# Layer B's last eight adaLN gate columns, made as sixteen half columns under the query projections

## The chip, the core and the metric

The kernel runs on one NeuronCore of one Trainium2 chip. The metric is device time in microseconds (us) of one launch. The kernel before took 1255.73 us in the median of three runs (1254.37, 1255.73, 1255.77).

## What is computed

A trunk of two layers on a sequence of 256 rows of width 2048, all in fp32. Layer A is a Mamba-2 mixer. Then one K and one V are projected for layer B, which is an attention over three head groups (dilations 1, 4 and 16) with its own queries and a SiLU gate path. Cut to what the change touches:

```python
for layer in range(2):
    shift, scale, gate = jnp.split(jax.nn.silu(c) @ ada_w[layer] + ada_b[layer], 3, axis=-1)
    h = x * (1.0 + scale) + shift
    y = _ssd_mixer(h, ...) if layer == 0 else _dilated_mixer(h, k_sh, v_sh, b_in_w[0], b_out_w[0])
    x = _layer_norm(4.0 ** 0.25 * x + (1.0 + gate) * y, ln_g[layer], ln_b[layer])
    if layer == 0:
        k_sh, v_sh = jnp.split(x @ kv_w, 2, axis=-1)     # 2048 -> 2 x 3072
```

The queries and z are `h @ b_in_w`, 2048 to 3072 + 1024. shift and scale are needed before the queries. gate is needed only behind the output projection, at the very end.

## The kernel before, in words

**A product.** Weights come from HBM in pieces of 128x1024 fp32 (512 KB). `load_piece` (L91) loads one into a buffer `raw`, of which there are six. `split` (L96) makes a high part `whi` on ScalarE (L99) and a low part `wlo` on VectorE (L101), four buffers each. TensorE multiplies both with the activations: `cm_wide` (L136) makes two 128-row tiles of K or of a query from four pieces, with matmuls of 512 columns on `whi` (L149) and 256 columns on `wlo` (L152); `tm_chunk` (L184) makes a 512-column stripe of V from eight pieces (L173 to L175). A buffer `raw` is free again when its `whi` and `wlo` are made, and the pair is free when TensorE has used it.

**adaLN.** A row of `ada_w` for 128 outputs, a column in the kernel's words, is a 128x2048 tile (1 MB) in one of two buffers `araw`. `ada_dot` (L246) multiplies it with silu(c) on VectorE (L251) and sums along the row, which gives one column of `mod`. Layer B has 48 columns: 16 pairs of scale and shift, then 16 of gate. `queue` (L269) turns a list of columns into background jobs: job i issues the load of column i+1 (L244) and then does the dot of column i. `background(n, every)` (L107) is called after each piece and runs n jobs per `every` pieces, so `rate` sets the mix. `gate_out` (L258) adds the bias to the gates, transposes them on TensorE (L262), copies the result on VectorE (L264) and stores it to DRAM (L265), from where the last stage reads it back spread over all partitions.

**The stages around the change.** Eleven of the 48 columns are done under layer A's output projection. The stage in `with tc.issue_after(tile4.ins)` makes the last V stripe of the first half, then the six K blocks (48 pieces), then three V stripes (24 pieces): 80 pieces in all, with R = (1, 2), one job per two pieces, for the other 37 columns and `gate_out(1)`. Then the activations are scaled and shifted in place (L828, L829, `split_act` L195), and `queries(0)` (L854), 24 pieces, makes the first half's queries. Under them run sixteen jobs `weigh` (L839), one per piece, which multiply the residual `u` with LayerNorm's g and add its b; each group of four loads 2x256 KB of `lnrow` spread over all partitions into one single buffer `pT` first. `attend(0)` (L861) and `queries(1)` follow and are interleaved on TensorE; in each of four heads come the scores (L874, L876), the bias (L880), the maximum (L883), the exponential on ScalarE (L885), its scaling (L887), the transposes (L890) and the product with V (L897, L900).

**What sets the order.** All loads are issued by one in-order queue, SP's. Every engine runs its instructions in the order in which the framework's list scheduler has put them; it lets an instruction move ahead of others where its own estimates and the buffers allow it. `issue_after(x)` keeps an instruction behind x.

Of the kernel before, what the change touches and what calls it, by code (L numbers as in the profile page):

```python
# [9 lines left out]
F32 = mybir.dt.float32  # L10
# [3 lines left out]
ALU = mybir.AluOpType  # L14
# [4 lines left out]
P = 128  # L19
L = 256  # L20
D = 2048
KT = D // P
# [7 lines left out]
EPS = 1e-5  # L30
SCALE = 128.0 ** -0.5
NEG = -1.0e30
SLOPES = [2.0 ** (-8.0 * n / 24.0) for n in range(1, 25)]


# [14 lines left out]
def trunk(ctx, tc, xT, x, c, par, cst, bias, lnrow, ada, wdt, win, wxs, wout, wk, wv, wbin, wbout, out):  # L50
    nc = tc.nc
    V, S, T, PO = nc.vector, nc.scalar, nc.tensor, nc.gpsimd

    cons = ctx.enter_context(tc.tile_pool(name="cons", bufs=1))
    wp = ctx.enter_context(tc.tile_pool(name="wp", bufs=3))
# [10 lines left out]
    cb_ = cons.tile([P, D], F32, name="cb_")  # L66
# [24 lines left out]
    def load_piece(src):  # L91
        raw = wp.tile([P, 1024], F32, name="raw", bufs=6)
        nc.sync.dma_start(raw, src)
        return raw
# [9 lines left out]
    jobs, latest, copied, pin = [], [], [], [None]  # L104

    def background(n, every=1):

        state[0] += n
        while state[0] >= every and jobs:
            state[0] -= every  # L110
            jobs.pop(0)()
# [17 lines left out]
    def acc_pair(pool=None):  # L129
        return [(pool or mm).tile([P, 2, L], F32, name="acc") for _ in range(2)]  # L130
# [8 lines left out]
    def cm_wide(src, dst, rate=(0, 1), moving=None):  # L139

        both, high = moving or (lambda kt: xp[:, kt], lambda kt: xhi[:, kt, :])
        ps = acc_pair()
        for q in range(KT // 4):
            hi, lo = (t.rearrange("p k n -> p (k n)").rearrange("p (k n) -> p k n", k=4)
                      for t in split(load_piece(src[q])))
            for k in range(4):
                kt = 4 * q + k
                for n in range(2):
                    T.matmul(ps[n], hi[:, k, n * P:n * P + P], both(kt), start=kt == 0, stop=False,  # L149
                             skip_group_check=True)  # L150
                for n in range(2):
                    T.matmul(ps[n][:, 0, :], lo[:, k, n * P:n * P + P], high(kt), start=False, stop=kt == KT - 1,  # L152
                             skip_group_check=True)
            background(*rate)
        for n in range(2):
            S.activation(dst[:, n, :], ps[n][:, 1, :], AF.Copy)
            V.tensor_tensor(dst[:, n, :], ps[n][:, 0, :], dst[:, n, :], op=ALU.add)

    def tiles(ps):
        return [ps[n // 2][:, n % 2, :] for n in range(4)]  # L160
# [71 lines left out]
    mod = [cons.tile([P, KT, 3], F32, name=f"mod{i}") for i in range(2)]  # L232
# [25 lines left out]
    def gate_out(layer):  # L258

        ada_bias(layer, slice(0, KT), slice(2, 3))  # L260
        pt = aux.tile([P, 512], F32, name="aux")[:KT, :P]
        T.transpose(pt, mod[layer][:, :, 2], ident)  # L262
        row = sm.tile([KT, P], F32, name="row", bufs=1)
        V.tensor_copy(row, pt)  # L264
        nc.sync.dma_start(gated[layer].rearrange("(k p) -> k p", p=P), row)  # L265

    def queue(pool, cols):

        loaded = [ada_load(pool, *cols[0])]  # L269

        def step(i):
            raw = loaded.pop(0)
            if i + 1 < len(cols):
                loaded.append(ada_load(pool, *cols[i + 1]))
            ada_dot(*cols[i], raw)

        jobs.extend(lambda i=i: step(i) for i in range(len(cols)))

    def drain():
        while jobs:  # L280
            jobs.pop(0)()
# [8 lines left out]
    with ExitStack() as cA:  # L290
# [14 lines left out]
        with ExitStack() as cS:  # L305
# [38 lines left out]
            def xs_wide(g):  # L344

                xs[g] = p0.tile([P, 4, L], F32, name="xs")
                for w in range(2):
                    t = xs[g][:, 2 * w:2 * w + 2, :]
                    cm_wide(wxs[2 * g - 4 + w], t, rate=R, moving=(lambda kt: hp[:, :, kt, :], hh_))
                    for n in range(2):  # L350
                        conv(t[:, n, :], 4 * g + 2 * w + n, t[:, n, :])

            def product(kind, g, pre=None):
# [7 lines left out]
                if kind == "z":  # L361
                    ps = tm_chunk(src, hh_, hl_, rate=R, k0=k0, pre=pre)
                    if g not in sz:
# [5 lines left out]
                    return  # L369
                ps = cm_quad(src, hhi, hlo, rate=R, k0=k0)  # L370
                t = tiles(ps)
# [9 lines left out]
            with ExitStack() as c0:  # L381
# [4 lines left out]
                raws, xts, late = [], {}, []  # L386
# [34 lines left out]
                part = {n: p[1:] for n, p in zip(names, begun.values())}  # L421
                two = "h"
                order = []
                for row in ("b4:0. b6:0. h z2:0. b2:0 x1:0 h", "b2:1. x1:1. z1:0 z1:1. z4:0 h h",
# [3 lines left out]
                    for w in row.split():  # L428
                        if w == two:
                            n = -2 if sum(o[0] == -2 for o in order) == sum(o[0] == -1 for o in order) else -1  # L430
# [98 lines left out]
            px = pe = cS.enter_context(tc.tile_pool(name="px", bufs=2, reuse_waits="tile"))  # L529
            R = (1, 10)  # L530

# [181 lines left out]
        cols1 = [(1, kind, kt) for kt in range(KT) for kind in ("scale", "shift")] + \  # L713
# [70 lines left out]
    with ExitStack() as cL:  # L784
        pl = cL.enter_context(tc.tile_pool(name="pl", bufs=3))

        vps = [tm_pair(), tm_pair()]
        for b in range(2):
            for kt in range(4):
                tile4 = x_tile(kt, (b,))  # L790
            for n in range(1, 4):
                normalise(b, 512 * n, 512 * n + 512)
            for i, w in enumerate(first_v):
                if b and i == 2:
                    x_tile(4)
                    x_tile(5)
                tm_mults(i // 2, w, vps[i % 2], hx, lx, 0, KT, (b,))
        for q in range(2, KT // 2):
            if q < KT // 2 - 1:
                x_tile(2 * q + 2)  # L800
                x_tile(2 * q + 3)
            for j in range(2):
                w = split(load_piece(wv[2 * j][q]), after=tile4.ins if q == 2 else None)
                tm_mults(q, w, vps[j], hx, lx, 0, KT, range(2))
        for g in range(2):
            evict_v(0, g, vps[g])

        R = (1, 2)
        pin[0] = latest[-1].ins
        with tc.issue_after(tile4.ins):  # L810
            state[0] = 0
            queue(pl, cols1[11:])
            jobs.append(lambda: gate_out(1))
            evict_v(0, 2, tm_chunk(wv[4], hx, lx, rate=R))
            for hq in range(2):
                for g in range(NG):
                    kv[hq, g] = place(3 + 3 * hq + g, [P, 4, L])
                    for w in range(2):
                        cm_wide(wk[2 * (2 * g + hq) + w], kv[hq, g][:, 2 * w:2 * w + 2, :], rate=R)
            for g in range(NG):  # L820
                evict_v(1, g, tm_chunk(wv[1 + 2 * g], hx, lx, rate=R))
            drain()
            late = latest[-1].ins

        ada_bias(1, slice(0, KT), slice(0, 2))
        for kt in range(KT):
            t = pl.tile([P, L], F32, name="htmp")
            S.activation(t, xhi[:, kt, :].bitcast(F32), AF.Identity, bias=shift(1, kt), scale=scale(1, kt))  # L828
            V.scalar_tensor_tensor(t, xlo[:, kt, :].bitcast(F32), scale(1, kt), t, op0=ALU.mult, op1=ALU.add)  # L829
            split_act(xhi[:, kt, :], xlo[:, kt, :], t)  # L830
    cQ = ctx.enter_context(ExitStack())
    pc2 = cQ.enter_context(tc.tile_pool(name="pc2", bufs=2))
# [5 lines left out]
    R = (0, 1)  # L838

    def weigh(n, b, i):  # L840
        if b == 0 and i == 0:
            t = pc2.tile([P, 1024], F32, name="pT", bufs=1)
            lnr[n] = [t[:, 512 * j:512 * j + 512] for j in range(2)]
            for j in range(2):
                bcast(lnr[n][j], lnrow, j * D + 512 * n)
        cs_ = slice(512 * n, 512 * n + 512)
        with tc.issue_after(late):
            V.tensor_tensor(u[b][:, cs_], u[b][:, cs_], lnr[n][i], op=(ALU.mult, ALU.add)[i])

    lnr = {}  # L850
    state[0] = 0
    jobs.extend(lambda n=n, b=b, i=i: weigh(n, b, i) for n in range(4) for i in range(2) for b in range(2))

    def queries(hq):  # L854
        qq = [pc2.tile([P, 4, L], F32, name=f"q{g}") for g in range(NG)]
        for g in range(NG):
            for w in range(2):
                cm_wide(wbin[2 * (2 * g + hq) + w], qq[g][:, 2 * w:2 * w + 2, :], rate=(1, 1))
        return qq

    def attend(hq, qq):  # L861

        for i in range(4):
# [3 lines left out]
            for g, c_ in enumerate((slice(0, 384), slice(384, 512), slice(512, 640))):  # L867
                V.scalar_tensor_tensor(bi[:, c_], dmat if g == 0 else dmat[:, P:2 * P], SLOPES[g * H + h], gmask[:, c_],
                                       op0=ALU.mult, op1=ALU.add)
# [59 lines left out]

    qs = [queries(0)]  # L930
    attend(0, qs[0])
    qs.append(queries(1))
    attend(1, qs[1])
    state[0] = 0
    jobs.extend(lambda i=i: hold(i, [hold_in(i, k) for k in range(2)]) for i in range(6))
# [102 lines left out]
def _layout(x, c, ada_w, ada_b, ln_g, ln_b, a_in_w, a_conv_w, a_conv_b, a_dt_bias,  # L1038
# [29 lines left out]
    def mask(delta, win_, dil):  # L1068
        return np.where((delta >= 0) & (delta % dil == 0) & (delta <= win_), 0.0, NEG)

# [37 lines left out]
```

## Time and profile before

| what | before |
|---|---|
| median of three runs | 1255.73 us |
| the profiled execution | 1254.31 us, of which the span is 1252.5 us |
| TensorE matmuls busy (PE) | 97% of the span |
| TensorE weight loads (PEld) | 83% |
| VectorE (DVE) | 82% |
| ScalarE (ACT) | 56% |
| mean rate of the DMAs | 268 GB/s |
| granted TensorE clock | 0.998 |

How to read it: times in the trace are counted from the start of the span. `L101` is line 101 of the kernel. A row of the timeline has start, duration, engine, line, operation, tiles, shapes and count, and in brackets the idle time of the engine just before it and what ended it. Durations of rows with x2 are from the first start to the last end.

### The profile page before, as it was taken

The numbers are of one execution on the slowest core, as the hardware profiler recorded it, in microseconds if no ns is written. First come the engines' busy times: TensorE is split into PE (matmuls) and PEld (weight loads), VectorE is DVE, ScalarE is ACT, GpSimd is POOL, SyncE is SP. The second block draws the span as 40 slices with busy tenths as digits, with TensorE's granted clock in tenths as the row PEclk, the third lists the DMA queues.
The fourth block names the chain that finished last, engine by engine and source line by source line (L and its number), as shares of the span: only waits on it lengthen the run. The fifth ranks groups of instructions, "written<-read, shape, count | busy, mean of one in ns | idle before, by whom it ended". The sixth has DMA issues, their size and how long they took to land.

```text
span 1252.5 us, 18746 instructions
## 1 busy us (share of the span) xinstructions
PE 1218.5 (97%) x7086; PEld 1042.7 (83%) x7086; DVE 1032.4 (82%) x1466; ACT 702.1 (56%) x1039; POOL 0.2 (0%) x4
## 2 busy tenths in 40 slices
PE   4999999999999999999999999999999999999997
PEld 4989998898888878788888788888888888888886
DVE  6999986999987989899777778879888866758777
ACT  3655577869588789653444444434445644445631
POOL 0000000000000000000000000000000000000000
PEclk9999999999999999999999999999999999999999
DMA  9999977677556546699898569989998774464741
GB/s 381 422 421 423 420 252 261 225 274 286 201 169 225 171 159 202 223 328 358 335 323 298 174 192 383 363 315 344 364 389 309 229 248 136 132 203 120 228 177 67
DMA packets 80586, 335.88 MB, mean 268 GB/s; under 512 B 9104, under 2 KB 9328, under 8 KB 67696
## 3 DMA queue, kind: packets, MB, share of 16 engines
q1 hardware_dynamic: 80496, 334.69, 73.9%
q8 instruction: 55, 0.90, 0.3%
q14 instruction: 35, 0.29, 0.1%
HBM read 332.47 MB, written 2.18 MB: 267 GB/s over the span
## 4 chain that ended last, share of the span: by engine, by line
PE 86%; DVE 5%; DMA 5%; issue 2%; ACT 1%; SPq 0%; DVEq 0%; ACTq 0%
PE acc L149 20%; PE acc L174 13%; PE acc L175 13%; PE acc L173 13%; PE acc L152 10%; PE acc L125 3%; PE acc L127 3%; PE acc L126 3%; DMA raw<-in_wk 2%; DVE wlo L101 1%; PE py L625 1%; DMA raw<-in_win 1%; DVE araw L251 1%; DMA araw<-in_ada 1%; DMA raw<-in_wv 1%
## 5 line engine op out<-in xcount | busy, mean ns | idle before, releaser
L99 ACT ACTIVATE whi<-raw 128x1024 fp32r<-128x1024 f32 x392 | 412.1, 1058 | 386.0 <-PE acc L175 151.4
L101 DVE TENSOR_TENSOR wlo<-raw,whi 128x1024 fp32r<-128x1024 f32 x392 | 473.5, 1221 | 145.3 <-ACT whi L99 141.1
L149 PE MATMUL acc<-actT,whi 128*128 128x512 f32 x1280 | 405.2, 397 | 0.0
L152 PEld LDWEIGHTS acc<-actT,wlo 128*128 128x128 f32 x1280 | 238.9, 188 | 62.8 <-DVE wlo L101 8.2
L174 PE MATMUL acc<-wlo,actT 128*128 128x512 f32 x688 | 270.0, 392 | 0.6 <-DVE wlo L101 0.5
L173 PE MATMUL acc<-whi,actT 128*128 128x512 f32 x688 | 266.6, 394 | 1.2 <-ACT actT L681 1.2
L152 PE MATMUL acc<-actT,wlo 128*128 128x256 f32 x1280 | 253.7, 280 | 4.5 <-DVE wlo L101 3.7
L251 DVE SCALAR_TENSOR_TENSOR araw<-araw,cb__72 128x2048 f32<-128x2048 f32 x96 | 219.3, 2285 | 9.5 <-DMA araw<-in_ada 9.3
L149 PEld LDWEIGHTS acc<-actT,whi 128*128 128x128 f32 x1280 | 195.8, 189 | 0.4
L175 PE MATMUL acc<-whi,actT 128*128 128x512 f32 x432 | 168.8, 391 | 0.0
L174 PEld LDWEIGHTS acc<-wlo,actT 128*128 128x128 f32 x688 | 129.3, 188 | 28.5 <-DVE wlo L101 2.8
L173 PEld LDWEIGHTS acc<-whi,actT 128*128 128x128 f32 x688 | 128.8, 188 | 27.2 <-ACT actT L681 1.7
L125 PE MATMUL acc<-actT,whi 128*128 128x256 f32 x384 | 108.9, 288 | 17.6 <-ACT actT L414 17.5
L126 PE MATMUL acc<-actT,whi 128*128 128x256 f32 x384 | 109.5, 287 | 0.0
L127 PE MATMUL acc<-actT,wlo 128*128 128x256 f32 x384 | 107.3, 287 | 1.2 <-DVE wlo L101 1.2
L175 PE MATMUL acc<-whi,ylo 128*128 128x512 f32 x256 | 100.7, 393 | 0.0
L175 PEld LDWEIGHTS acc<-whi,actT 128*128 128x128 f32 x432 | 81.1, 188 | 16.6
L125 PEld LDWEIGHTS acc<-actT,whi 128*128 128x128 f32 x384 | 74.3, 194 | 18.6 <-ACT actT L414 17.7
L126 PEld LDWEIGHTS acc<-actT,whi 128*128 128x128 f32 x384 | 75.1, 196 | 0.3
L127 PEld LDWEIGHTS acc<-actT,wlo 128*128 128x128 f32 x384 | 73.9, 196 | 1.6 <-DVE wlo L101 1.6
L175 PEld LDWEIGHTS acc<-whi,ylo 128*128 128x128 f32 x256 | 48.1, 188 | 9.7
L583 ACT ACTIVATE seg<-cbc,cumT 128x128 f32<-128x128 f32 x128 | 41.2, 389 | 5.0 <-PE py L625 4.9
(257 smaller groups left out, 1061.7 us busy)
## 6 DMA issues: line engine op xcount, KB each, us to landing
araw<-in_ada SPq DMA_DIRECT2D x96, 1024.0 KB, 7.3
raw<-in_win SPq DMA_DIRECT2D x112, 512.0 KB, 6.1
raw<-in_wout SPq DMA_DIRECT2D x64, 512.0 KB, 5.2
raw<-in_wbin SPq DMA_DIRECT2D x64, 512.0 KB, 4.2
raw<-in_wxs SPq DMA_DIRECT2D x48, 512.0 KB, 4.5
raw<-in_wv SPq DMA_DIRECT2D x48, 512.0 KB, 5.9
raw<-in_wk SPq DMA_DIRECT2D x48, 512.0 KB, 8.0
cbc<-cumd SPq DMA_DIRECT2D x16, 512.0 KB, 5.1
```

The source lines that it names most:

```text
L99: copied.append(S.activation(hi, raw, AF.Copy))
L101: latest.append(V.tensor_tensor(lo, raw, hi.bitcast(F32), op=ALU.subtract))
L125: T.matmul(o, hi[:, k, c_], ahi[:, kt, :], start=first, stop=False, skip_group_check=True)
L126: T.matmul(o, hi[:, k, c_], alo[:, kt, :], start=False, stop=False, skip_group_check=True)
L127: T.matmul(o, lo[:, k, c_], ahi[:, kt, :], start=False, stop=kt == k1 - 1, skip_group_check=True)
L149: T.matmul(ps[n], hi[:, k, n * P:n * P + P], both(kt), start=kt == 0, stop=False, skip_group_check=True)
L152: T.matmul(ps[n][:, 0, :], lo[:, k, n * P:n * P + P], high(kt), start=False, stop=kt == KT - 1, skip_group_check=True)
L173: T.matmul(o, h_, hi[:, k, :], start=kt == k0, stop=False, skip_group_check=part)
L174: T.matmul(o, h_, lo[:, k, :], start=False, stop=False, skip_group_check=part)
L175: end = T.matmul(o, l_, hi[:, k, :], start=False, stop=kt == k1 - 1, skip_group_check=part)
L251: V.scalar_tensor_tensor(raw, raw, 1.0, cb_, op0=ALU.mult, op1=ALU.mult, accum_out=mod[layer][:, ct, j:j + 1])
L583: S.activation(seg[:, hh, b, :], cbc[:, hh, b, :], AF.Relu, bias=cumT[:, b, h0 + hh:h0 + hh + 1], scale=-1.0)
```

## The change

The last eight of the sixteen gate columns leave the list of the K and V stage, and `gate_out(1)` with them. The other 29 columns of that stage run at R = (2, 5), two jobs per five pieces instead of one per two. The eight columns are loaded as sixteen halves of 128x1024 (512 KB) into the weight pieces' six buffers `raw`. Their jobs `half_dot` each issue the load of the next half and do the dot of their own. Eight of them stand between the `weigh` jobs of `queries(0)`, one after every two, so the `weigh` jobs now take 24 pieces; the other eight and `late_gates`, which adds the two partial sums and calls `gate_out(1)`, run in `queries(1)` with one job per two pieces. What is computed stays the same. Line numbers of the changed kernel are one higher up to L806, and about 26 higher from `queries` on.

```diff
+LATE = 8
...
-        R = (1, 2)
+        R = (2, 5)
         pin[0] = latest[-1].ins
         with tc.issue_after(tile4.ins):
             state[0] = 0
-            queue(pl, cols1[11:])
-            jobs.append(lambda: gate_out(1))
+            queue(pl, cols1[11:-LATE])
...
+    part = pc2.tile([P, LATE, 2], F32, name="part", bufs=1)
+    coming = []
+
+    def half_load(i):
+        raw = wp.tile([P, 1024], F32, name="raw", bufs=6)
+        nc.sync.dma_start(raw, ada[1, 2, KT - LATE + i // 2][:, 1024 * (i % 2):1024 * (i % 2) + 1024])
+        coming.append(raw)
+
+    def half_dot(i):
+        if i == 0:
+            half_load(0)
+        if i + 1 < 2 * LATE:
+            half_load(i + 1)
+        raw = coming.pop(0)
+        with tc.issue_after(late):
+            V.scalar_tensor_tensor(raw, raw, 1.0, cb_[:, 1024 * (i % 2):1024 * (i % 2) + 1024], op0=ALU.mult,
+                                   op1=ALU.mult, accum_out=part[:, i // 2, i % 2:i % 2 + 1])
+
+    def late_gates():
+        V.tensor_tensor(mod[1][:, KT - LATE:, 2], part[:, :, 0], part[:, :, 1], op=ALU.add)
+        gate_out(1)
+
     state[0] = 0
-    jobs.extend(lambda n=n, b=b, i=i: weigh(n, b, i) for n in range(4) for i in range(2) for b in range(2))
-
-    def queries(hq):
+    todo = [lambda n=n, b=b, i=i: weigh(n, b, i) for n in range(4) for i in range(2) for b in range(2)]
+    halves_ = [lambda i=i: half_dot(i) for i in range(2 * LATE)]
+    for i in range(8):
+        jobs.extend([*todo[2 * i:2 * i + 2], halves_[i]])
+    jobs.extend([*halves_[8:], late_gates])
+
+    def queries(hq, rate=(1, 1)):
...
-                cm_wide(wbin[2 * (2 * g + hq) + w], qq[g][:, 2 * w:2 * w + 2, :], rate=(1, 1))
+                cm_wide(wbin[2 * (2 * g + hq) + w], qq[g][:, 2 * w:2 * w + 2, :], rate=rate)
...
-    qs.append(queries(1))
+    qs.append(queries(1, (1, 2)))
+    drain()
```

SP's queue in the K projection before, with `raw` the weight pieces and `araw` the columns:

```order
L93 DMA raw_7573<-in_wk 128x1024
L93 DMA raw_7595<-in_wk 128x1024
L244 DMA araw_7617<-in_ada 128x2048
L93 DMA raw_7620<-in_wk 128x1024
L93 DMA raw_7642<-in_wk 128x1024
L244 DMA araw_7664<-in_ada 128x2048
```

and the same place of the queue now:

```order
L94 DMA raw_7570<-in_wk 128x1024
L94 DMA raw_7592<-in_wk 128x1024
L245 DMA araw_7614<-in_ada 128x2048
L94 DMA raw_7617<-in_wk 128x1024
L94 DMA raw_7639<-in_wk 128x1024
L94 DMA raw_7667<-in_wk 128x1024
L245 DMA araw_7689<-in_ada 128x2048
```

A column stood between every two pieces, and stands now in turn behind two and behind three.

VectorE at the start of `queries(0)` before: `wlo` are the low parts of the query weights, the rows with `u` are `weigh`, and the rows with `q0` evict the first two query tiles.

```order
L101 TENSOR_TENSOR wlo_9457<-raw_9454,whi_9456 128x1024
L868 SCALAR_TENSOR_TENSOR bi_9944<-bs_9342 128x384
...
L848 TENSOR_TENSOR u0_5509<-u0_5509,pT_9375 128x512
L848 TENSOR_TENSOR u1_5510<-u1_5510,pT_9375 128x512
...
L101 TENSOR_TENSOR wlo_9483<-raw_9480,whi_9482 128x1024
L101 TENSOR_TENSOR wlo_9506<-raw_9503,whi_9505 128x1024
L101 TENSOR_TENSOR wlo_9529<-raw_9526,whi_9528 128x1024
L157 TENSOR_TENSOR q0_9348<-acc_9351,q0_9348 128x256
...
L848 TENSOR_TENSOR u0_5509<-u0_5509,pT_9476 128x512
```

The same place now, where the rows with `part` are the halves:

```order
L866 SCALAR_TENSOR_TENSOR raw_9395,part_9314<-raw_9395,cb__72 128x1024
L102 TENSOR_TENSOR wlo_9432<-raw_9429,whi_9431 128x1024
L866 SCALAR_TENSOR_TENSOR raw_9397,part_9314<-raw_9397,cb__72 128x1024
L102 TENSOR_TENSOR wlo_9455<-raw_9452,whi_9454 128x1024
L866 SCALAR_TENSOR_TENSOR raw_9474,part_9314<-raw_9474,cb__72 128x1024
L848 TENSOR_TENSOR u0_5509<-u0_5509,pT_9346 128x512
L848 TENSOR_TENSOR u1_5510<-u1_5510,pT_9346 128x512
...
L158 TENSOR_TENSOR q0_9319<-acc_9322,q0_9319 128x256
...
L102 TENSOR_TENSOR wlo_9480<-raw_9477,whi_9479 128x1024
L102 TENSOR_TENSOR wlo_9506<-raw_9503,whi_9505 128x1024
L866 SCALAR_TENSOR_TENSOR raw_9554,part_9314<-raw_9554,cb__72 128x1024
L848 TENSOR_TENSOR u0_5509<-u0_5509,pT_9499 128x512
```

Three halves have come ahead of the first group of `weigh`, and that group stands now behind the low part of the sixth piece (`wlo_9455`), where it stood behind that of the fifth.

VectorE in the first head of `attend(0)` before, with `sc0` and `sc1` the scores of the two row blocks, `nm` their maximum and `den` the sums of the exponentials:

```order
L883 TENSOR_REDUCE nm_9954<-sc0_9948 128x1
L883 TENSOR_REDUCE nm_9973<-sc1_9967 128x1
L868 SCALAR_TENSOR_TENSOR bi_9995<-bs_9342 128x384
...
L886 RECIPROCAL den_9956<-den_9956 128x1
L887 TENSOR_SCALAR sc0_9948<-sc0_9948,den_9956 128x512
L886 RECIPROCAL den_9975<-den_9975 128x1
L887 TENSOR_SCALAR sc1_9967<-sc1_9967,den_9975 128x512
```

and now:

```order
L909 TENSOR_REDUCE nm_9951<-sc0_9945 128x1
L909 TENSOR_REDUCE nm_9970<-sc1_9964 128x1
L894 SCALAR_TENSOR_TENSOR bi_9992<-bs_9312 128x384
...
L866 SCALAR_TENSOR_TENSOR raw_10340,part_9314<-raw_10340,cb__72 128x1024
L912 RECIPROCAL den_9953<-den_9953 128x1
L913 TENSOR_SCALAR sc0_9945<-sc0_9945,den_9953 128x512
L912 RECIPROCAL den_9972<-den_9972 128x1
L913 TENSOR_SCALAR sc1_9964<-sc1_9964,den_9972 128x512
```

One half stands now between the maximum and the scaling of the first head; the next one (`raw_10393`) stands likewise ahead of the scaling of the fourth head.

## The prediction

> **What bounds the kernel now.** I read the page first, for the engine that is busiest, then the table of stretches by stage, then what TensorE's weight loads wait for, since a busy PE can hide waits.
>
> ```profile
> PE 1218.5 (97%) x7086; PEld 1042.7 (83%) x7086; DVE 1032.4 (82%) x1466; ACT 702.1 (56%) x1039; POOL 0.2 (0%) x4
> ```
>
> PE is busy 97% of the span, so only the places where it stands still can give anything back. The change touches the K and V stage and the queries. These are the stretches from the start of K to the end of `queries(1)`: us, then busy time with counts in the order PE, PEld, DVE, ACT, POOL, then clock, DMA share and GB/s.
>
> ```profile
> 776.00:843.00 67.00, 67.00 (x387) 58.44 (x386) 53.27 (x54) 26.41 (x34) 0.00 (x0) 1.00 0.90 345
> 843.00:912.00 69.00, 67.32 (x379) 56.83 (x378) 60.21 (x64) 29.57 (x39) 0.00 (x0) 1.00 0.95 357
> 912.00:979.00 67.00, 66.83 (x293) 53.96 (x292) 57.16 (x72) 39.25 (x58) 0.00 (x0) 1.00 0.87 331
> 979.00:999.00 20.00, 20.00 (x115) 17.37 (x114) 14.32 (x20) 10.63 (x15) 0.00 (x0) 1.00 0.73 218
> 999.00:1019.00 20.00, 19.29 (x109) 16.24 (x108) 14.86 (x19) 8.52 (x11) 0.00 (x0) 1.00 0.77 234
> 1019.00:1050.00 31.00, 31.00 (x181) 27.16 (x181) 17.74 (x20) 13.85 (x18) 0.00 (x0) 1.00 0.69 233
> 1050.00:1081.00 31.00, 31.00 (x203) 27.57 (x201) 28.34 (x65) 15.39 (x32) 0.00 (x0) 1.00 0.28 89
> 1081.00:1132.00 51.00, 51.00 (x295) 44.52 (x294) 25.96 (x28) 22.35 (x27) 0.00 (x0) 1.00 0.60 191
> ```
>
> The first two rows hold the same work, K. In the first, PE does 387 matmuls in 67 us, 5.776 per us, and never stops. At that rate 69 us would hold 398.6; the second row has 379. The 19.6 that are missing are 3.4 us. Row five has 109 where 20 us would hold 115.5: 1.1 us. The waits of the weight loads say for what, in these three windows (843 to 912, 912 to 960, 1000 to 1020; total, times, longest):
>
> ```profile
> PEld acc L152 <- DVE wlo L101: 4.3, 6, 1.4
> ...
> PEld acc L174 <- DVE wlo L101: 1.7, 4, 0.5
> ...
> PEld acc L152 <- DVE wlo L101: 1.6, 2, 0.8
> ```
>
> TensorE waits for the low parts that VectorE makes, and in the K and V stage at a steady beat:
>
> ```profile
> 849.07 0.30 PEld L152 LDWEIGHTS acc<-actT,wlo 128*128 128x128 f32 x2 [0.59 <-DVE wlo L101]
> 860.63 0.30 PEld L152 LDWEIGHTS acc<-actT,wlo 128*128 128x128 f32 x2 [0.58 <-DVE wlo L101]
> 872.99 0.30 PEld L152 LDWEIGHTS acc<-actT,wlo 128*128 128x128 f32 x2 [1.38 <-DVE wlo L101]
> ```
>
> Six waits of 4.3 us cost 3.4 us, so about 0.15 us of each is the ordinary spacing of two loads. The four of the V stripes then cost 1.7 - 4 x 0.15 = 1.1 us. Together the K and V stage loses 4.5 us and the queries 1.1 to 1.3.
>
> Why is VectorE late? A piece is 16 matmuls, 16 / 5.776 = 2.77 us, and 0.524 MB; a column is 1.049 MB. Two pieces and a column per 5.54 us are 2.097 MB, a need of 378 GB/s. The rows above deliver 345 and then 357 GB/s, the latter with the DMAs 0.95 busy. In the first 67 us the stage lives on what was loaded ahead: 67 x (378 - 345) = 2.2 MB, four pieces of the six buffers. From 843 us on the lead is gone. SP's queue adds to it: it issues a column only when a buffer is free, and the weights stand behind it.
>
> ```profile
> SPq L244 <- DVE araw L251: 145.5, 34, 7.5
> ```
>
> That is 145.5 us of SP waiting between 740 and 1050 us for the dot of an earlier column.
>
> **K and V stage: columns at two per five pieces.** The need falls to 5 x 0.524 + 2 x 1.049 = 4.72 MB per 13.85 us, 341 GB/s, a tenth less and just under what both stretches delivered. VectorE: the dots are 2285 ns and an accumulator read of 82 ns each.
>
> ```profile
> L251 DVE SCALAR_TENSOR_TENSOR araw<-araw,cb__72 128x2048 f32<-128x2048 f32 x96 | 219.3, 2285 | 9.5 <-DMA araw<-in_ada 9.3
> L101 DVE TENSOR_TENSOR wlo<-raw,whi 128x1024 fp32r<-128x1024 f32 x392 | 473.5, 1221 | 145.3 <-ACT whi L99 141.1
> ...
> L251 DVE DVE_READ_ACCUMULATOR araw<-araw,cb__72 128x1 f32 x34 | 2.8, 82 | 0.0
> ```
>
> Between 843 and 912 us stand 12 of them; a fifth fewer is 2.4 x 2.37 = 5.7 us, so DVE falls from 60.21 to 54.5 us of 69, 79%: the share of the first row (53.27 of 67), in which nothing waits. The last of the 29 jobs comes at piece 73 of 80, as the 37th did at 74, so the conversion of the activations behind it keeps its place. What could be late next there is the supply itself, 341 against 345 to 357 GB/s. Bounds for this term: nothing gone (0) to all gone (-4.5 us); I take **-4.5**, because the lead now lasts: even at 331 GB/s, the lowest of the three rows, the shortfall of 10 GB/s over 204 us is 2.0 MB, which the lead of four pieces covers.
>
> The store of the gates leaves this stage too. SP stood 10.7 us at it with the last weights of V behind it, and PE did not notice (row three loses only the 1.1 us above). I give nothing for it.
>
> ```profile
> SPq L265 <- DVE row L264: 10.7, 1, 10.7
> ```
>
> **First queries: eight halves, and `weigh` spread out.** The loss of 1.1 to 1.3 us comes from `weigh`: VectorE stands at it until its `lnrow` has landed, and the next `wlo` is behind it.
>
> ```profile
> 1003.94 1.29 DVE L848 TENSOR_TENSOR u<-u,pT 128x512 f32<-128x512 f32 x2 [1.17 <-DMA pT<-in_lnrow]
> 1006.65 0.69 DVE L848 TENSOR_TENSOR u<-u,pT 128x512 f32<-128x512 f32 x1 [1.41 <-DMA pT<-in_lnrow]
> 1007.26 1.22 DVE L101 TENSOR_TENSOR wlo<-raw,whi 128x1024 fp32r<-128x1024 f32 x1
> ...
> 992.43 0.80 SPq L63 DMA_DIRECT2D pT<-in_lnrow  x2
> 993.56 2.60 SPq L93 DMA_DIRECT2D raw<-in_wbin  x3
> 1000.53 1.44 SPq L63 DMA_DIRECT2D pT<-in_lnrow  x2
> ```
>
> With one buffer `pT`, load, `weigh` and next load form a ring that takes 1000.53 - 992.43 = 8.1 us and has four pieces, 11.1 us, at one job per piece. The jobs take one and a half times the pieces now, so the ring has 16.6 us, and the order puts 4 to 5 us of other work (two or three `wlo`, a half, the evictions) between a group's end and the next group's start. This wait should go: **-1.1** (bounds -1.3 and, if the halves only take its place, 0).
>
> The halves themselves: no such instruction is in the trace. Above, it costs like a `wlo` of the same 1024 columns plus the accumulator read, 1.30 us; below, half a dot plus the read, 1.22. I take 1.30. Eight are 10.4 us, so DVE between 979 and 1050 us goes from 46.9 to 57.3 us of 71. DMA: in the first 40 us, 9.0 MB moved at a share of 0.75; five halves add 2.6 MB and the last `lnrow` group (0.5 MB) moves out, so the share rises to 0.92. Full, but not over; and since a half uses one of the six buffers, the weights run about four pieces, 11 us, ahead, against 4.2 us for a piece to land:
>
> ```profile
> araw<-in_ada SPq DMA_DIRECT2D x96, 1024.0 KB, 7.3
> ...
> raw<-in_wbin SPq DMA_DIRECT2D x64, 512.0 KB, 4.2
> ```
>
> I take 0 for the halves here; without that cover, each half that delays a piece costs 0.524 MB at 299 GB/s (218 / 0.73), 1.75 us.
>
> The Trainium skill speaks against halves: its page "DMA: Bandwidth & Descriptors" asks in the section Bandwidth for transfers of 1 MiB or more, and gives in Anatomy of one DMA a fit, made on GpSimd's path, of about 2.0 us plus bytes / 436e3 for each. By it, as an estimate, sixteen halves would take 51 us one after another where eight columns take 35; if all of that showed, the sum would be 16 us worse. The trace agrees in direction (7.3 us for 1024 KB, 4.2 for 512), but not that it adds up: 357 GB/s were moved with both sizes in flight at once.
>
> **First attention: halves on a full VectorE.** Between 1050 and 1081 us DVE is busy 28.34 of 31 us, and two halves (2.6 us) come in. The one of the first head stands ahead of its scaling, with nothing else behind which it could hide:
>
> ```profile
> 1048.92 1.23 DVE L101 TENSOR_TENSOR wlo<-raw,whi 128x1024 fp32r<-128x1024 f32 x1 [1.56 <-PE aux L876]
> 1050.06 0.75 DVE L157 TENSOR_TENSOR q<-acc,q 128x256 f32<-128x256 f32 x2
> ...
> 1053.11 0.95 DVE L868 SCALAR_TENSOR_TENSOR bi<-bs 128x384 f32<-128x384 f32 x3
> 1053.98 0.16 DVE L886 RECIPROCAL den<-den 128x1 f32<-128x1 f32 x1
> ...
> 1054.76 0.49 DVE L887 TENSOR_SCALAR sc<-sc,den 128x512 f32<-128x512 f32 x1
> ...
> 1055.65 0.60 PE L890 MATMUL po<-cc,sc 128*128 128x128 f32 x4
> ```
>
> Scaling ends at 1055.25. PE comes to the first transposes at 1055.65, and by the changed order 0.4 us later, so there are 0.4 to 0.8 us of room. Its turn would be 1053.98. Its load stands behind that of a piece whose buffer the `wlo` of 1048.92 frees at 1050.15; issued at about 1050.5 and 4.2 us on its way, it lands at 1054.7. The scaling then ends 0.7 + 1.3 = 2.0 us later, less the room of 0.8 and another 0.5 since the two row blocks are transposed one after the other: **+0.7 us** (bounds 0, if the load is there, and 2.0 with no room). In the fourth head PE has some 3 us of query matmuls ahead of the transposes, which cover the other half. The gate's transposes, its copy and its store come late in `queries(1)`, before a stage that reads the store some 60 us later: 0.
>
> **Sum.** -4.5 - 1.1 + 0.7 = **-4.9 us**: the profiled execution of 1254.31 us would be 1249.4. The three runs are at 1254.4, 1255.7 and 1255.8, so that execution lies near the lowest; from their mean of 1255.3 I forecast **1250.4 us**.
>
> **Rivals.** (1) The waits under the queries only change their place: DMA at 0.92, `weigh` 0 instead of -1.1 and attention at 1.6: -2.9, 1252.4 us. For it: the share; against: four pieces of lead. (2) The change doesn't do what it says: VectorE's waits stay, since 341 GB/s is hardly less than what came, and only the queries gain: -1.1 + 0.7 = -0.4, 1254.9 us. For it: the first row moved no more than 345; against: it did so while SP waited for dots, and without PE losing anything. (3) Slower: VectorE stands at halves that have not landed, in order, with the softmax behind them. In `queries(1)` loads alternate two pieces and a half, and the half's buffer waits for the sixth load before it. If three halves under the attention are issued only as their turn comes, each costs landing plus dot, 4.2 + 1.3, less 0.8 of room: 3 x 4.7 = 14.1, less 5.6: +8.5, 1263.8 us. It decides from two such halves on (9.4 against 5.6). Against: the lead of two to four pieces by the order. By the fixed share of each DMA that the Trainium skill's page gives (Anatomy of one DMA), a half would land in more than half of a column's time.
>
> **How the numbers follow.** Forecast 0.58, rival (1) 0.18, (2) 0.12, (3) 0.12. The bound for "the same" is 0.2%, 2.5 us, about what a measurement can tell here: 1253.2 to 1258.2. Forecast counts as faster but for 0.02; of (1), 0.8 us from the bound, 0.13 is faster; (2) is the same; (3) slower: 0.69, 0.19, 0.12. The range: below, 1254.4 - 5.8 with all waits gone from the fastest run and nothing paid, 1248.6, rounded down to 1248.2 for that spread; above, (2) with the spread of the runs, 1256.0. It leaves out (3).
>
> **What would show it.** K and V: no wait of PEld for `wlo` between 843 and 960 us, SP's waits for dots mostly gone, DMA share under 0.93. Queries: no wait at L153 for L102 of over 0.3 us; if there are some, VectorE idle ahead of `weigh` or of a half tells (1). Attention: PE waiting some 0.7 us ahead of the first head's transposes (L916), behind a DVE that waits for a DMA of `raw`; more of these tell (3). The forecast is wrong if VectorE waits for ScalarE's `whi`, and that for DMAs, in K as before.

## The result, and the profile after

The changed kernel takes **1257.82 us** (median of 9 runs, 1256.48 to 1261.43), the kernel before in the same series 1255.55 us (9 runs, 1252.85 to 1256.15): a ratio of 1.003, 95% interval 1.0021 to 1.004. It is a little slower; 1250.4 had been forecast, and 1257.82 lies above the range given (1248.2 to 1256.0). The profiled execution took 1261.43 us, the slowest of its nine, with a span of 1259.7 us.

TensorE's busy time is where it was; the span around it has grown by 7.2 us.

```profile
PE 1218.8 (97%) x7086; PEld 1045.5 (83%) x7086; DVE 1034.4 (82%) x1483; ACT 703.5 (56%) x1039; POOL 0.2 (0%) x4
```

The stretches answer to those of before (us; busy time and counts of PE, PEld, DVE, ACT, POOL; clock, DMA share, GB/s):

```profile
843.00:912.00 69.00, 69.00 (x398) 60.21 (x397) 56.49 (x61) 31.28 (x40) 0.00 (x0) 1.00 0.94 340
912.00:979.00 67.00, 67.00 (x300) 55.56 (x299) 50.55 (x63) 38.70 (x58) 0.00 (x0) 1.00 0.76 250
999.00:1019.00 20.00, 20.00 (x117) 17.47 (x116) 17.14 (x25) 9.83 (x13) 0.00 (x0) 1.00 0.89 339
1019.00:1050.00 31.00, 30.08 (x174) 25.89 (x173) 22.14 (x30) 13.99 (x18) 0.00 (x0) 1.00 0.86 289
1050.00:1081.00 31.00, 25.67 (x153) 22.69 (x152) 25.87 (x56) 10.78 (x23) 0.00 (x0) 0.89 0.46 145
```

K gained what was promised: 398 matmuls in 69 us instead of 379, and TensorE no longer stops. Row three does not stop either. But the last row, with the first head of the attention in it, holds 153 matmuls instead of 203: TensorE is idle for 5.3 us, and even the clock falls.

Windows of fixed times mix the stages, since this execution was 4.0 us late before the change begins. So I counted TensorE's 7086 matmuls in both traces and took the time from one count to another. These stages are used in all that follows:

| stage (matmuls) | before | changed | difference |
|---|---|---|---|
| first layer and start of K and V (1 to 4751) | 800.8 | 804.8 | +4.0 |
| the rest of K and V (to 5501) | 146.3 | 141.7 | **-4.6** |
| most of `queries(0)` (to 5751) | 48.2 | 47.6 | -0.6 |
| end of `queries(0)`, first head (to 6001) | 43.8 | 52.1 | **+8.4** |
| the next thousand (to 7001) | 174.8 | 174.6 | -0.2 |

In the stages that the change touches, that is -4.6 - 0.6 + 8.4 - 0.2 = +3.0 us, near the 2.3 us by which the medians differ. The 4.0 us of the first row come ahead of the change, where both programs have the same instructions and addresses; they are looked at below.

What TensorE's weight loads wait for between 1000 and 1066 us (total, times, longest):

```profile
PEld aux L900 <- DVE sc L906: 5.8, 1, 5.8
PEld acc L153 <- DVE wlo L102: 1.6, 2, 1.4
```

It is one wait above all. TensorE's matmuls stand for 5.3 us at it and for 0.9 us at the `wlo`; with the half clock behind the wait (last section), that is most of the 8.4 us. The scores of the second head (L900, into `aux`) need a buffer in PSUM, the memory that TensorE writes to, which is free when VectorE has taken the scores of the first head out of it (L906). Why VectorE is late stands in the chain of waits of that stretch, in order of time (start, us, what):

```profile
1031.23 3.41 DVE wlo L102 x3
...
1034.66 6.93 DMA raw<-in_ada
...
1041.68 0.23 DVE raw L866
...
1042.95 3.79 DMA raw<-in_ada
...
1046.83 0.12 DVE raw L866
...
1048.09 4.45 DMA raw<-in_ada
...
1052.63 0.12 DVE raw L866
...
1053.87 1.14 DVE wlo L102
1055.00 0.67 DVE q L158 x2
1055.67 0.61 DVE sc L906
...
1056.32 1.22 PE aux L900 x2
```

Read it from the bottom: the scores (`sc`) stand behind the last eviction of the queries (`q`), this behind a half's multiplication (L866), this behind the half's DMA, and that DMA was issued when **the half before it** was done: load, half, load, half. Between 1034.66 and 1052.54 us the chain is on the way through DMAs for 15.2 of 17.9 us. VectorE's own rows say that it stood idle for 8.0 us at these three halves:

```profile
1041.68 1.23 DVE L866 SCALAR_TENSOR_TENSOR raw<-raw,cb__72 128x1024 f32<-128x1024 f32 x1 [4.76 <-DMA raw<-in_ada]
1042.84 0.08 DVE L866 DVE_READ_ACCUMULATOR raw<-raw,cb__72 128x1 f32 x1
...
1046.83 1.22 DVE L866 SCALAR_TENSOR_TENSOR raw<-raw,cb__72 128x1024 f32<-128x1024 f32 x1 [0.97 <-DMA raw<-in_ada]
...
1052.63 1.23 DVE L866 SCALAR_TENSOR_TENSOR raw<-raw,cb__72 128x1024 f32<-128x1024 f32 x1 [2.29 <-DMA raw<-in_ada]
```

and SP's queue that each load begins as the row above ends (the accumulator of the first is read out at 1042.92):

```profile
1042.95 0.33 SPq L856 DMA_DIRECT2D raw<-in_ada  x1
1044.78 1.43 SPq L94 DMA_DIRECT2D raw<-in_wbin  x2
1048.09 0.33 SPq L856 DMA_DIRECT2D raw<-in_ada  x1
```

Two things of the program make this ring. In the code the halves nine to twelve belong to pieces of `queries(1)`, but on VectorE they stand ahead of the last evictions of `queries(0)`, since nothing there holds them back. And the pool gives each of them not the sixth buffer in turn but the one that has just come free, which is that of the half before: in the built program the halves ten to thirteen all have one address (as have seven to nine, and fourteen to sixteen).

### The profile page after: what moved, and what is told of

It is laid out like the page before. It is cut to its first block, busy times and chain, and to the rows that moved or that the text cites. A ratio compares the mean times of both kernels' runs of the same rounds, so it can differ in the third digit from the quotient of the medians.

```text
span 1259.7 us, 18753 instructions
## 1 busy us (share of the span) xinstructions
PE 1218.8 (97%) x7086; PEld 1045.5 (83%) x7086; DVE 1034.4 (82%) x1483; ACT 703.5 (56%) x1039; POOL 0.2 (0%) x4
## 4 chain that ended last, share of the span: by engine, by line
PE 82%; DMA 7%; DVE 6%; ACT 3%; issue 2%; SPq 0%; DVEq 0%; ACTq 0%
PE acc L150 20%; PE acc L176 12%; PE acc L175 12%; PE acc L174 12%; PE acc L153 10%; PE acc L126 3%; PE acc L128 3%; PE acc L127 3%; DMA raw<-in_ada 2%; DMA araw<-in_ada 2%; DMA raw<-in_wbin 2%; DVE wlo L102 2%; PE py L626 1%; ACT whi L100 1%; DVE araw L252 1%
## 5 line engine op out<-in xcount | busy, mean ns | idle before, releaser
L252 DVE SCALAR_TENSOR_TENSOR araw<-araw,cb__72 128x2048 f32<-128x2048 f32 x88 | 201.1, 2285 | 11.7 <-DMA araw<-in_ada 11.5
```

Of the source, the lines that this page charges most:

```text
L252: V.scalar_tensor_tensor(raw, raw, 1.0, cb_, op0=ALU.mult, op1=ALU.mult, accum_out=mod[layer][:, ct, j:j + 1])
```

## The experiments

Three theories were on the table. **A**: VectorE, in order, stands at halves that are still on their way, with evictions and scores behind them. **B**: the DMA engines are full with the halves (0.89 and 0.86 above, where before had 0.77 and 0.69), and the weights are late. **C**: VectorE has too much to do. All times are medians, with the ratio to the kernel before in the same series (1254.9 to 1255.9 us) and its 95% interval; the stage from matmul 5751 to 6001 ("end of the queries" below) is 43.8 us before and 52.1 in the changed kernel.

**No halves: K and V alone.**

```diff
-        V.tensor_tensor(mod[1][:, KT - LATE:, 2], part[:, :, 0], part[:, :, 1], op=ALU.add)
+        V.memset(mod[1][:, KT - LATE:, 2], 0.0)
...
-    for i in range(8):
-        jobs.extend([*todo[2 * i:2 * i + 2], halves_[i]])
-    jobs.extend([*halves_[8:], late_gates])
+    jobs.extend([*todo, late_gates])
```

> The part in K and V alone: two of the other gate columns per five weight pieces, and no halves at all; the last eight gate columns are left out (zeros stand in their place). The kernel before has a median of 1255.55 us, the changed one 1257.82. All theories put the gain of K and V at 4 to 5 us, so 1251 (1249.5 to 1252.5). If the time is 1254 or more instead, the 4.6 us that the trace shows won in K and V do not reach the end, and the loss is not that of the halves alone.

Measured 1253.47 us, ratio 0.9982 (0.9968 to 0.9996): faster, but 1 us above the upper end of what was expected. The trace has the 4.6 us in K and V, in full; the end of the queries takes 44.4 us, with one wait of 1.6 us for a `wlo` behind `weigh`, which is one job per piece again. The gain of K and V reaches the end, so the loss is that of the halves.

**Multiplications without loads, and loads without multiplications.** The first reads the condition's vector twice, the second has GpSimd read one column of each half:

```diff
-        nc.sync.dma_start(raw, ada[1, 2, KT - LATE + i // 2][:, 1024 * (i % 2):1024 * (i % 2) + 1024])
...
-            V.scalar_tensor_tensor(raw, raw, 1.0, cb_[:, 1024 * (i % 2):1024 * (i % 2) + 1024], op0=ALU.mult,
+            V.scalar_tensor_tensor(raw, cb_[:, :1024], 1.0, cb_[:, 1024 * (i % 2):1024 * (i % 2) + 1024], op0=ALU.mult,
```

```diff
-        with tc.issue_after(late):
-            V.scalar_tensor_tensor(raw, raw, 1.0, cb_[:, 1024 * (i % 2):1024 * (i % 2) + 1024], op0=ALU.mult,
-                                   op1=ALU.mult, accum_out=part[:, i // 2, i % 2:i % 2 + 1])
+        PO.tensor_copy(part[:, i // 2, i % 2:i % 2 + 1], raw[:, :1])
```

> The halves' sixteen multiplications stay on VectorE, each in a buffer of the weight pieces, but they read the condition's vector twice and no half is loaded (the last eight gate columns are left out of the result). Theory A, VectorE stands at halves that have not landed, and theory B, the DMA engines are full: the loss of about 8 us goes, 1249 to 1252 us. Theory C, the sixteen times 1.3 us of added work on a VectorE that is full under the attention: most of the loss stays, 1256 to 1258 us.

> The halves are loaded at the same places into the same buffers, but VectorE does nothing with them: GpSimd reads one column of each, which sets the buffer free (the last eight gate columns are left out of the result). Theory A (VectorE in order stands at a half, with evictions and softmax behind it): the loss goes, 1249 to 1252 us. Theory B (8.4 MB more for DMA engines that were full between 1010 and 1030 us, weights late for PE): the loss stays, 1256 to 1259. Theory C (VectorE's work): it goes as by A.

Loads alone: 1250.28 us, 0.9962 (0.9949 to 0.9974). Multiplications alone: 1256.15 us, 1.0007 (0.9995 to 1.0019). By the times alone theory C would have won. The traces say otherwise. First the stretch in question, in the kernel with multiplications alone, then in that with loads alone:

```profile
1010.00:1062.00 52.00, 52.00 (x304) 45.37 (x303) 41.88 (x64) 23.80 (x32) 0.00 (x0) 1.00 0.70 229
```

```profile
1010.00:1062.00 52.00, 52.00 (x314) 45.66 (x314) 35.93 (x60) 24.65 (x38) 2.89 (x9) 1.00 0.78 268
```

TensorE does not stop in either. Eight multiplications (9.85 us) are done in this stretch in the first kernel, as many as in the changed one, and its end of the queries takes 43.0 us: VectorE's work costs nothing there. TensorE came to this stretch 6 us late in this kernel, which could hide some of that work; but twelve halves with two buffers, below, have the same work ahead of the same scores as twelve with one, and take 44.1 us where those take 50.2. So C falls as the main cause. In the second the loads are made, at a DMA share of 0.78, and the stage takes 43.0 us as well: B falls as far as TensorE is concerned. The first kernel's time went elsewhere, to its first query pieces:

```profile
PEld acc L150 <- ACT whi L100: 3.5, 1, 3.5
```

```profile
SPq L835 <- DVE actT L199: 18.3, 1, 18.3
```

Without the halves' loads, the load of the attention's bias came to stand ahead of four weight pieces in SP's queue, and SP stood at it for 18.3 us. That kernel was a poor control, since taking away the loads also moved what stood behind them; only its stretch from 1010 us on could be used.

**The second eight behind the first attention.** Nothing is left out; the multiplications nine to sixteen may not stand ahead of the last instruction of `attend(0)` on VectorE:

```diff
-    coming = []
+    coming, attended = [], []
...
-        with tc.issue_after(late):
+        with tc.issue_after(late if i < 8 else attended[0]):
...
-            V.tensor_copy(qq[0][:, i, :], po)
+            attended[:] = [V.tensor_copy(qq[0][:, i, :], po).ins]
```

> The whole change, but the multiplications of the second eight halves are queued on VectorE behind the last instruction of the first attention; nothing is left out. Theory A: no half stands ahead of the softmax any more, so most of the 8.4 us lost between 1043 and 1061 us come back: 1249.5 to 1252.5 us. Theory B: the first eight halves and the full DMA engines between 1010 and 1030 us are as before, and half of the loss or more stays: 1254 to 1258. Theory C: as A, since the work leaves the attention too, but with some waits of PE behind it.

> The version with eight halves ahead and eight behind the first attention once more, beside the other two: 1250 to 1251.5 us, 4 to 5.5 us under the kernel before, with no wait of TensorE over 0.3 us between 815 and 1100 us.

Measured 1250.82 us, 0.9956 (0.9939 to 0.9972), and in the repetition 1250.10 us, 0.996 (0.9946 to 0.9974). In the repetition TensorE does not stop in the whole stretch:

```profile
1010.00:1062.00 52.00, 52.00 (x310) 45.51 (x309) 40.20 (x65) 26.03 (x39) 0.00 (x0) 1.00 0.71 243
```

The end of the queries takes 43.0 us in both. In the repetition the halves nine to twelve are loaded about as early as in the changed kernel (the ninth lands at 1032.7 us, there at 1034.4), and VectorE takes them from 1078.7 us on. This version is faster than both kernels. By the same count of matmuls as above, it gains 6.2 us over the first profile of the kernel before and 4.8 us over the second (below); the medians are 4.5 and 5.8 us apart.

**The changed kernel once more, and eleven or twelve ahead.** The changed kernel has no edit; the others have the edit above with 11 or 12 in place of 8:

```diff
-        with tc.issue_after(late if i < 8 else attended[0]):
+        with tc.issue_after(late if i < 11 or not attended else attended[0]):
```

> The changed kernel once more, beside the other three, for a second profile: 1256.5 to 1259 us. Theory A (VectorE stands at halves that are still on their way, with the evictions of the last query columns and the first scores behind them): TensorE again loses 7 to 9 us between 1040 and 1062 us and some 4.6 us less than before in K and V. If the loss is at another place this time, theory A is not what sets the time.

> As with the second eight halves behind the first attention, but only the last five are put there: eleven stand ahead of the first scores instead of twelve in the changed kernel and eight in that one, and none in the first head. Nothing is left out. Theory A: each half ahead of the scores costs a round of 5 to 6 us (landing and multiplication) once VectorE has no other work to do meanwhile; without the twelfth and thirteenth the eviction that TensorE waits for at 1050.6 us comes some 5 us earlier, so that 1 to 2.5 us of the 8.4 are left: 1251 to 1254 us. If all thirteen cost alike (0.65 us each), 1256 or more.

> As with eleven ahead, but twelve halves stand ahead of the first scores, as many as in the changed kernel; the thirteenth, which there stands in the first head, and the last three are behind the attention. Nothing is left out. With eight ahead the median was 1250.8 us, with eleven 1251.0, with twelve and one in the first head 1258.7. Theory A (the twelfth is the first whose round of landing and multiplication, 5.9 us in the trace, finds no cover): 1256 to 1258.5 us, so the half in the first head costs 0 to 2. If the half in the first head made the loss: 1251 to 1253.

| halves ahead of the first scores | end of the queries | median | ratio (95%) |
|---|---|---|---|
| eight | 43.0, 43.0 | 1250.8, 1250.1 | 0.9956, 0.9960 |
| eleven | 43.8 | 1251.0 | 0.9967 (0.9957 to 0.9977) |
| twelve | 50.2 | 1257.2 | 1.001 (0.9995 to 1.0025) |
| twelve, and one in the first head (changed kernel) | 52.1, 50.5 | 1257.8, 1258.7 | 1.003, 1.0027 (1.0015 to 1.0038) |

TensorE's first score matmuls of the second head, with eleven and then with twelve ahead:

```profile
1049.36 0.70 PE L900 MATMUL aux<-s,q 128*128 128x256 f32 x2 [0.64 <-DVE sc L906]
```

```profile
1055.70 1.22 PE L900 MATMUL aux<-s,q 128*128 128x256 f32 x2 [5.51 <-DVE sc L906]
```

In its second profile the changed kernel stands at the same place again, for 5.25 us. The halves do not cost alike: eleven cost 0.8 us together, the twelfth alone 6.4. Of these, 4.9 us are the longer wait (5.51 instead of 0.64), nearly a round of the ring (5.2 to 5.8 us, the distance of the rows of L866 above); the rest goes with the half clock behind it (last section). So a round is free as long as VectorE is ahead of TensorE by more than that, and then costs nearly all of itself. The half in the first head adds 0.3 us by the second profile of the changed kernel (50.5 against 50.2); of the 1.6 us more in its first profile, 0.9 are TensorE standing at a `wlo` ahead of the scores.

**Two buffers in turn.** With thirteen ahead (the order that came out of it) and, together with the edit above, with twelve:

```diff
-    coming = []
+    coming, pair = [], []
...
-        raw = wp.tile([P, 1024], F32, name="raw", bufs=6)
+        if i < 2:
+            pair.append(wp.tile([P, 1024], F32, name="raw", bufs=6))
+        raw = pair[i % 2]
```

> The halves take two fixed buffers of the six in turn, in place of one that each gets from the half ahead of it; the weight pieces keep four; nothing is left out. On VectorE one half more than in the changed kernel stands ahead of the first scores (thirteen instead of twelve). Theory A1, the loss comes from the load that may start only when the half ahead of it is done (4 to 5 us of landing in each round): the landing is hidden, 1250 to 1253 us. Theory A2, the halves stand too early on VectorE, however they are buffered: 1256 to 1260 us, with VectorE again waiting for their DMAs.

> Twelve ahead and four behind the attention, but with two fixed buffers for the halves in turn (four are left to the weights). Nothing is left out. With thirteen ahead and two buffers TensorE waited 3.9 us before the first scores, and halves followed each other at 3.2 to 3.9 us in place of 5.0 to 5.9. Theory A1 (the length of a round decides, so the single buffer is a part of the cause): one round less leaves 0 to 1.5 us of waiting, 1251 to 1253.5 us, at least 3 less than twelve with one buffer. Theory A2 (only the number of halves ahead of the scores decides): the same time as twelve with one buffer, 1256 to 1258.5.

With thirteen 1255.04 us, 1.0005 (0.9993 to 1.0018), above what A1 gave and just under A2; with twelve 1254.34 us, 0.9988 (0.9977 to 1.0), 2.9 us under twelve with one buffer, again between the two. In the traces the end of the queries takes 49.3 us with thirteen and 44.1 with twelve, where twelve with one buffer takes 50.2. They differ more than the times because each is one execution, and these lie at the ends of their series: twelve with one buffer took 1260.27 us (1251.65 to 1260.29), twelve with two 1251.04 (1249.9 to 1256.91), thirteen 1259.11, the slowest of its twelve. The same first scores as above, with thirteen and then with twelve:

```profile
1053.67 1.22 PE L902 MATMUL aux<-s,q 128*128 128x256 f32 x2 [3.73 <-DVE sc L908]
```

```profile
1048.29 0.70 PE L902 MATMUL aux<-s,q 128*128 128x256 f32 x2 [0.93 <-DVE sc L908]
```

So the single buffer is a part of the cause (at twelve halves 6.2 us between these two traces, 2.9 us between the medians; with thirteen and two buffers the median is 3.6 us under that of the changed kernel beside it, 1258.7), but not all of it. From the ninth half to the twelfth, with twelve ahead, one takes 3.7 us on the average with two buffers and 5.7 with one, and not zero, and one half more brings the wait back. What counts by these traces is rounds times their length against the time that VectorE has until the first scores.

**The halves alone, K and V undone.** All columns whole in K and V at one per two pieces, and the halves made once more under the queries:

```diff
-        R = (2, 5)
+        R = (1, 2)
...
-            queue(pl, cols1[11:-LATE])
+            queue(pl, cols1[11:])
+            jobs.append(lambda: gate_out(1))
...
-        gate_out(1)
```

> The other part alone: K and V make all gate columns, one per two pieces, as in the kernel before, and the sixteen halves are made once more under the queries as in the changed kernel (their sums are not used). If the parts add up, the loss of 7.8 us (8.4 less 0.6) stands without the gain of 4.6: 1262 to 1265 us. If the halves' loss hangs on the shorter K and V (their later start would find VectorE less pressed), 1257 to 1260.

Measured 1260.0 us, 1.0034 (1.002 to 1.0049). The parts do not add up: K and V take 146.3 us as before (the 4.6 us are lost again), but the end of the queries only 47.4 us instead of 50.5 to 52.1. A slower K and V brings TensorE to the scores later, while the ring does not come later by as much: matmul 5751 starts 4.9 and 5.7 us later than in the two profiles of the changed kernel, the twelfth half only 1.7 and 3.8 us later. By this reading, 3 to 5 of the 4.6 us won in K and V only bring TensorE sooner to a VectorE that is still busy with its ring. That this explains all of the difference is not shown, since VectorE's order differs too: an eviction stands ahead of the tenth half here and behind it there.

**The kernel before once more.**

> The kernel before once more, for a second profile of it. In all eleven profiled runs of changed versions the first layer, whose instructions are the same as before, ended 1.4 to 4.4 us later than in the one profile of the kernel before. If that is a scatter between executions, TensorE's 4751st matmul starts at 817 to 821 us here too; if the changed versions are slower there, it starts at 815 to 816.5 as in the first profile. In K and V TensorE loses the same 4.6 us as in the first profile, and in the queries the same 1.1 to 1.4: 1254 to 1257 us.

Measured 1255.19 us. Its 4751st matmul starts at 815.7 us, as in the first profile, and its K and V take 146.3 us, the same to 0.05 us. But the queries lose nothing this time:

```profile
962.00:1010.00 48.00, 48.00 (x253) 41.09 (x252) 40.98 (x66) 31.65 (x51) 0.00 (x0) 1.00 0.80 262
1010.00:1062.00 52.00, 52.00 (x312) 45.57 (x311) 34.94 (x55) 24.52 (x36) 0.00 (x0) 1.00 0.60 192
```

The end of the queries is 43.1 us here, not 43.8. VectorE waits for `lnrow` for 8.1 us between 975 and 1066 us, about as in the first profile (7.9 us), and TensorE does not notice. On the first layer the answer is the second of the two expected; what can be said of it stands at the end of the next section.

## Why the prediction was wrong, step by step

- **K and V, -4.5 us: right.** 4.6 us in every profile with the new rate, eleven of them, and 0.0 in the one with the old rate. No wait for `wlo` is left between 843 and 960 us, and SP's waits for dots of columns fell to 29.1 us (740 to 960 us). The DMA share of 0.94 was to be under 0.93.
- **The gate's store, 0: right.** Nothing in the stages shows it.
- **`weigh`, -1.1 us: mis-sized.** The wait was that of one execution. In the changed kernel it is gone, but in the second profile of the kernel before TensorE does not lose it either. The term is worth 0 to 1.4 us, depending on the execution.
- **The halves under the first queries, 0: the step that failed.** The text took "four pieces, 11 us, ahead, against 4.2 us for a piece to land" from the weights and let it stand for the halves too. The halves have no such lead. Each of the later ones gets the buffer of the half ahead of it, so it is asked for only when that is done, and lands 3.8 to 6.9 us later. Up to matmul 5751 this costs nothing; from there on it cost the changed kernel 7.5 and 9.1 us in its two profiles against the version with eight ahead. The order of VectorE, in which four halves of `queries(1)` stand ahead of the last eviction of `queries(0)`, was there to be read; only the DMA share and VectorE's sum were looked at, and the runs on theories B and C show that neither was the limit.
- **The first head, +0.7 us: mis-sized.** It looked for the loss at the half inside the head, which adds 0.3 us. The loss is one instruction group earlier, ahead of the scores.
- **Rival (3) was the right mechanism**, with a chance of 0.12, and its rule "it decides from two such halves on" is near to what was found (one is enough, the twelfth). Its buffer was not right (not that of the sixth load before but of the last half), nor its place (ahead of the first scores, not under the softmax), and its price of 14.1 us was 7.5 to 9.1.
- The rule of the Trainium skill against halves (DMA: Bandwidth & Descriptors, section Bandwidth) did not set the time: with all sixteen loads and no multiplication TensorE loses nothing. What the halves cost here is their landing, and that only where VectorE stands at each one.

What stays open: all profiles of changed versions are 1.4 to 4.4 us slower than both profiles of the kernel before in the first layer, with the same instructions. Both executions of before lie under their medians (1254.31 and 1252.89 us against 1255.7 and 1255.2), so this may be scatter; the part of it that shows is a column of that layer which in some executions lands late, with VectorE standing at it (2.2 us in the changed kernel), and the clock: in nine of the twelve profiles of changed versions it is half for 3.4 us once between 465 and 715 us, in neither profile of the kernel before. The kernel before is not always so fast: its 97 executions beside the experiments took 1252.15 to 1258.95 us, and 35 of them had a mean clock of 0.997 or less, where its two profiles have 0.998 and 0.999. Whether the changed versions meet these delays more often was not settled, nor how much of them is in the medians. That is why the stages, which repeat to 0.05 us in K and V, were used to tell the theories apart.

## What to carry to other kernels

A prefetch is as early as the release of the buffer that it is given, not as early as its place in the code: ask for every load of a background job whose buffer it takes, and what that one waits for. Work that an in-order engine takes from a DMA is not background work if what the busiest engine waits for stands behind it; count rounds (landing plus work) against the time until then, rather than adding up busy shares. Eight of the sixteen halves, queued behind the attention by a small edit, turned +0.3% into -0.4%.

## What the runs showed of the hardware

A wait of TensorE can cost more than its length. In the changed kernel the granted clock (the third column from the right) falls during the wait of 5.3 us and is half behind it:

```profile
1052.00:1056.00 4.00, 0.00 (x0) 0.00 (x0) 3.37 (x6) 0.00 (x0) 0.00 (x0) 0.79 0.81 278
1056.00:1060.00 4.00, 3.68 (x13) 3.32 (x14) 4.00 (x10) 1.52 (x4) 0.00 (x0) 0.50 0.64 212
```

The twelve score matmuls behind the wait take 3.4 us in the second profile of the changed kernel and 1.75 us with eight halves ahead: 1.7 us on top. The first pair of L900 or L902 behind the wait takes 1.22 us after waits of 3.73 and 5.51 us, and 0.70 us after 0.64 and 0.93 us.

No single length of a wait decides, though. With the halves alone TensorE waits 3.13 us and the first pair behind it still takes 0.70 us, but the clock falls 1.5 us later:

```profile
1057.99 0.70 PE L900 MATMUL aux<-s,q 128*128 128x256 f32 x2 [3.13 <-DVE sc L906]
```

```profile
1058.00:1062.00 4.00, 4.00 (x19) 3.71 (x20) 3.96 (x10) 1.73 (x5) 0.00 (x0) 0.68 0.48 176
```

In the first layer TensorE stands still for 2.07 to 2.08 us near 466 us in all fourteen profiles. In seven of them the clock is half for 3.4 us right behind that, in the other seven, among them both of the kernel before, it is not. The same stretch in the kernel before and then in the second profile of the changed kernel:

```profile
466.00:472.00 6.00, 4.92 (x28) 4.34 (x29) 5.75 (x10) 5.98 (x12) 0.00 (x0) 1.00 0.62 199
```

```profile
466.00:472.00 6.00, 4.91 (x19) 4.28 (x20) 5.76 (x10) 5.95 (x11) 0.00 (x0) 0.72 0.64 199
```

The Trainium skill (TensorE: Matmul & The Clock Gate, Part 1: The HAM clock gate) says that the clock falls to half after an idle window of about 3.4 us. The waits of 3.73 us and more agree with that; the fall behind waits of 3.13 and 2.08 us does not, so that here a shorter wait was enough in some executions.
